# Hybrid decoder layer on one Trainium2 core: the last attention block is normalised ahead of a scan and two gelus, and the output projection starts three chunks at once

## The chip, the cores and the metric

The kernel runs on one core of one Trainium2 chip. That core has five engines with a queue each: TensorE (PE, with its weight loads shown as PEld), VectorE (DVE), ScalarE (ACT), GpSimd (POOL) and SyncE (SP), which here only issues transfers. [...] The metric is the time of one execution in microseconds of the device.

## The reference

One layer: a half-step SwiGLU FFN, a token mixer made of two channel groups that run side by side, and a second half-step FFN, each between two RMS norms. The change lies in the mixer, at the place where its two groups come together:

```python
def rg_lru(x_in, ...):
    xc = causal_depthwise_conv(x_in, conv_w, conv_b)
    r = sigmoid(block_diag(xc, w_rg, b_rg)); i = sigmoid(block_diag(xc, w_ig, b_ig))
    log_a = LRU_C * r * log_sigmoid(lam)
    a = exp(log_a);  u = sqrt(-expm1(2.0 * log_a)) * (i * xc)
    h = associative_scan(h_t = a_t * h_{t-1} + u_t)          # along the sequence

y_lru  = rg_lru(x_lru, ...) * gelu(gate_lru)                  # 512 channels
y_attn = sliding_window_sink_attention(q, k, v, sinks)        # 512 channels, 8 heads of 64, blocks of 128
y = concatenate([rms_norm(y_lru, g_lru_out), rms_norm(y_attn, g_attn_out)])
return y @ w_o                                                # 1024 -> 1024
```

Sizes: 512 tokens, 1024 channels, FFN width 2816, one layer, float32.

## The kernel before

Activations lie transposed, 128 channels on the partitions by 512 tokens, one tile per chunk of channels. A float32 product is made of three passes of TensorE: weight and activation are each split into a high part (rounded by a ScalarE copy or activation) and a low part (the difference, made by VectorE or GpSimd), and high by high, high by low and low by high are summed in a bank of PSUM. `x_high` (line 431) and `x_low` (line 434) do this for an activation, and the planner `Weights` does it for weights: `W.take()` hands out a split weight, `W.fill(n)` splits ahead, and the next raw weight is fetched when the last user of a raw buffer has been issued. One low part of the output weight, `Deferred` (line 157), is written down at once but issued later by hand, with `deferred.run()`. The order on all five engines is the order of the program's calls.

The mixer's middle runs in ten steps, `now` from 0 to 9. There are eight units (block `b` of 128 queries, `n` one of two groups of four heads); in step `now` unit `now` gets its scores and exponentials, unit `now - 1` its transposed probabilities (`turn_p`), and unit `now - 2` its product with the values (`values`). With `n == 1` `values` ends a block: the reciprocal of the softmax sums (line 1268), the scaled output `yn` of the block (line 1271, from PSUM), and, deferred by `later` to a `run_due`, the sum of its squares on ScalarE (line 1273). Between these steps `pump(n)` puts pieces of the gate's projection `gt0` to `gt3` on TensorE, and the recurrent group's elementwise work goes on: `root`, `root_u`, the four `scan(ci)` (line 1172, VectorE), and the gelu of gate chunk `ci` in four parts: `gelu_a` scales it by the RMS factor (line 1012) and squares it (line 392), `gelu_b` makes the inner polynomial (lines 1120 and 1121), `gelu_c` the tanh (line 1124), `gelu_d` the product (line 1128, tile `G`). `G` exists for chunks 0 and 1; for 2 and 3 the product with the gate and that with 1 + tanh (`gated`, line 1354) stand apart.

Behind the loop, in the kernel before: `invert_rms` turns the sums of squares into 1/rms, by a root on ScalarE (line 1278, which needs another table of functions than tanh and exp), a reciprocal (line 1279) and one VectorE multiplication per block (line 1281); `turn_y` puts 16 TensorE transposes of the four normalised blocks into four banks `atp` (line 1331) and splits each bank into `yah` and `yal`; GpSimd multiplies the scans by the gates (line 1357); `gated` and `add_square` (lines 1342 and 1344) make the sum of squares `acc_lru`, which `lrms.stats()` takes to TensorE (line 406). `wo_attn(c)` (lines 1374 to 1377) starts output chunk `c` of `w_o` with the attention half alone: per chunk eight passes with `yah` and four with `yal`. Three chunks come ahead of `lrms.stats()`, two behind it; the recurrent half follows when its norm is known (line 1392 and line 361 on).

`preload(f)` is an activation on one dummy column that makes ScalarE load a table early (line 337).

Of the kernel before, what the change touches and what calls it, by code (L numbers as in the profile page):

```python
# [9 lines left out]
F32R = mybir.dt.float32r  # L10
U8 = mybir.dt.uint8
AF = mybir.ActivationFunctionType
# [3 lines left out]
P = 128  # L16
T = 512
NB = T // P
D = 1024
KD = D // P  # L20
F = 2816
FC = F // P
C = 512
KC = C // P
# [9 lines left out]
PUMPS = [(2, 1)] * 8 + [(1, 1), (1, 0), (4, 0)]  # L34
# [77 lines left out]
def tile_layer(ctx: ExitStack, tc: tile.TileContext, out: bass.AP, **ins: bass.AP):  # L112
    nc = tc.nc
    pe, dve, act, pool, sync = nc.tensor, nc.vector, nc.scalar, nc.gpsimd, nc.sync
# [10 lines left out]
    ALL = slice(0, T)  # L125
    HALF = [slice(0, T // 2), slice(T // 2, T)]

    def bank(name):
        return psum.tile([P, T], F32, tag="bank", name=name)

    def t2k(name, dt=F32):
        return big.tile([P, T], dt, tag="t2k", name=name, bufs=NT2K)

    def wt(name, w=T, dt=F32):
        return tmp.tile([P, w], dt, tag="w", name=name, bufs=NW)
# [184 lines left out]
    ident = const.tile([P, P], F32, name="ident")  # L320
# [11 lines left out]
    eps = filled("eps", 1, EPS)  # L332
# [3 lines left out]
    def preload(func):  # L336
        act.activation(dummy, eps, func)
# [9 lines left out]
    def col(name, i):  # L347
        return colrange(name)[:, i:i + 1]
# [41 lines left out]
    def square(src, sl, name):  # L390
        sq = wt(f"sq_{name}")[:, sl]
        act.activation(sq, src, AF.Square)  # L392
        return sq
# [36 lines left out]
    def x_high(x, src, gain, sl):  # L430
        act.activation(x[0][:, sl], src, AF.Copy, scale=gain)

    def x_low(x, src, gain, sl):
        dve.scalar_tensor_tensor(x[1][:, sl], src, gain, x[0].bitcast(F32)[:, sl], op0=ALU.mult, op1=ALU.subtract)
# [359 lines left out]
    ws = [w_tiles(KD, P, f"first{i}") for i in range(2)]  # L794
# [37 lines left out]
    tps = turn_early()  # L832
# [3 lines left out]
    banks = [bank(f"a_first{i}") for i in range(4)]  # L836
# [44 lines left out]
    tps = {c: turn(1, c) for c in range(0, KD, 2)}  # L881
# [87 lines left out]
    for g, (f0, f1) in enumerate(GROUPS1):  # L969
# [3 lines left out]
        for c in range(KD):  # L973
# [19 lines left out]
            b = pair_banks[c] if c < 2 else product(W.take(), xs, name=f"ya{g}{c}")  # L993
# [17 lines left out]
    def scaled(t, b):  # L1011
        dve.tensor_mul(t, b, R)
        return t
# [68 lines left out]
    for j in range(4):  # L1082
        b = in_product(f"pq{j}")
# [14 lines left out]
    Gs = {}  # L1098
# [3 lines left out]
    def later(i, fn, *args):  # L1102
        todo.append((i, fn, args))

    def run_due(i):
        nonlocal todo
        due, todo = [t for t in todo if t[0] <= i], [t for t in todo if t[0] > i]
        for _, fn, args in due:
            fn(*args)


    gts, gqs = {}, {}
# [5 lines left out]
    def gelu_b(ci):  # L1118
        sq = gqs[ci]
        dve.tensor_scalar(sq, sq, GC * GA, GC, op0=ALU.mult, op1=ALU.add)  # L1120
        (dve if ci else pool).tensor_mul(sq, sq, gts[ci])

    def gelu_c(ci):
        act.activation(gqs[ci], gqs[ci], AF.Tanh)
# [21 lines left out]
    now = 0  # L1146
    steps = fill_steps()

    def pump(n):
        for _ in range(n):  # L1150
            next(steps, None)
# [11 lines left out]
    def root(ci):  # L1163
        act.activation(th[ci], th[ci], AF.Sqrt)
# [4 lines left out]
    hl = us_  # L1169

    def scan(ci):
        dve.tensor_tensor_scan(hl[ci], rs_[ci], us_[ci], initial=0.0, op0=ALU.mult, op1=ALU.add)


    scale = HD ** -0.5
    yns = []
    ssq = const.tile([P, NB], F32, name="ssq")
# [76 lines left out]
    def values(b, n):  # L1254
        pc, pp = unit[b, n]
        if n == 0:
            unit[b, "o"] = bank(f"po{b}")
        po = unit[b, "o"]
        for j in range(4):
            hs = slice(j * P, (j + 1) * P)  # L1260
            o = po[:, (4 * n + j) * HD:(4 * n + j + 1) * HD]
            if b > 0:
                pe.matmul(o, pp[:, hs], v[:, (b - 1) * P + n * HD:(b - 1) * P + (n + 1) * HD], start=True, stop=False)
            pe.matmul(o, pc[:, hs], v[:, b * P + n * HD:b * P + (n + 1) * HD], start=b == 0, stop=True)
        if n == 0:
            return
        rden = small.tile([P, 8], F32, tag="rden", name=f"rden{b}")
        dve.reciprocal(rden, unit[b])
        yn = t2k(f"yn{b}")
        h8 = lambda t: t.rearrange("p (h d) -> p h d", h=8)  # L1270
        dve.tensor_mul(h8(yn), h8(po), rden.unsqueeze(2).to_broadcast([P, 8, HD]))
        yns.append(yn)
        later(now, lambda: act.activation(wt(f"junk{b}"), yn, AF.Square, accum_out=ssq[:, b:b + 1]))

    rat = const.tile([P, NB], F32, name="rat")

    def invert_rms(bs):
        act.activation(rat[:, bs], ssq[:, bs], AF.Sqrt, bias=eps, scale=1.0 / C)
        dve.reciprocal(rat[:, bs], rat[:, bs])
        for b in range(NB)[bs]:  # L1280
            dve.tensor_scalar(yns[b], yns[b], rat[:, b:b + 1], None, op0=ALU.mult)
# [6 lines left out]
    for now in range(n_units + 2):  # L1288
        if now < n_units:
            scores(*units[now])  # L1290
            if now in FILLS:
                W.fill(FILLS[now])
        pump(PUMPS[now][0])
        if 0 <= now - 1 < n_units:
            turn_p(*units[now - 1])
        if now < n_units:
            exps(*units[now])
        if now == 0:
            deferred.run()
        run_due(now - 1)  # L1300
        pump(PUMPS[now][1])
        if 0 <= now - 2:
            values(*units[now - 2])
        if now == 5:
            for ci in range(KC):
                root(ci)
            preload(AF.Exp)
        if now == 6:
            for ci in range(KC):
                root_u(ci)  # L1310
            for ci in (2, 3):
                scan(ci)
        if now == n_units:
            scan(0)
            deferred.run()
            scan(1)
            gelu_b(2)
            gelu_c(2)


    pump(PUMPS[-1][0])
    invert_rms(slice(0, NB - 1))
    run_due(n_units + 1)
    invert_rms(slice(NB - 1, NB))
    ysp = [None] * KD

    def turn_y():
        tps = [bank(f"atp{ci}") for ci in range(KC)]
        for b in range(NB):
            for ci in range(KC):  # L1330
                pe.transpose(tps[ci][:, b * P:(b + 1) * P], yns[b][:, ci * P:(ci + 1) * P], ident)
        for ci, tp in enumerate(tps):
            ysp[ci + KC] = t2k(f"yah{ci}", F32R), t2k(f"yal{ci}", F32R)
            x_high(ysp[ci + KC], tp, col("g_attn_out", ci), ALL)
            x_low(ysp[ci + KC], tp, col("g_attn_out", ci), ALL)


    accl = tmp.tile([P, T], F32, tag="acc", name="acc_lru", bufs=3)
# [1 line left out]
    def add_square(ci):  # L1340
        if ci == 0:
            act.activation(accl, hl[0], AF.Square)
        else:
            dve.tensor_add(accl, accl, square(hl[ci], ALL, f"l{ci}"))

    pump(100)
    gts[KC - 1] = scaled(wt(f"gt{KC - 1}"), gts[KC - 1])
    turn_y()
    gqs[KC - 1] = square(gts[KC - 1], ALL, f"g{KC - 1}")
    preload(AF.Exp)  # L1350
    gelu_b(KC - 1)

    def gated(ci):
        dve.scalar_tensor_tensor(hl[ci], gqs[ci], 1.0, hl[ci], op0=ALU.add, op1=ALU.mult)

    for ci in range(KC):
        pool.tensor_mul(hl[ci], hl[ci], Gs[ci] if ci in Gs else gts[ci])
    gated(2)
    for ci in (0, 1):
        add_square(ci)  # L1360
    gelu_c(3)
    gated(3)
    for ci in (2, 3):
        add_square(ci)
    preload(AF.Sqrt)
    lrms = [InvRms([accl], mean_c, h, f"lru{h}", eps4) for h in range(2)]
# [1 line left out]
    res = Residual("r2", lambda c: col("mix_post_g", c))  # L1368
    EARLY = KD - LATE

    def wo_attn(c):
        (hi, lo), ks = ws[c], range(KC, KD)
        for k in ks:
            pe.matmul(banks[c], hi[:, k, :], ysp[k][0], start=k == KC, stop=False)
            pe.matmul(banks[c], lo[:, k, :], ysp[k][0], start=False, stop=False)
        for k in ks:
            pe.matmul(banks[c], hi[:, k, :], ysp[k][1], start=False, stop=False)

    ws, banks = [], []
    for c in range(EARLY):  # L1380
        ws.append(W.take(0))
        banks.append(bank(f"wo{c}"))
        wo_attn(c)
        if c == EARLY - 3:
            for l in lrms:
                l.stats()
            W.fill(3)
        if c == EARLY - 2:
            bcs = [l.spread() for l in lrms]
            for ci in range(KC):  # L1390
                for h in range(2):
                    dve.tensor_mul(hl[ci][:, HALF[h]], hl[ci][:, HALF[h]], bcs[h])
                y = t2k(f"ylh{ci}", F32R), t2k(f"yll{ci}", F32R)
                x_high(y, hl[ci], col("g_lru_out", ci), ALL)
                x_low(y, hl[ci], col("g_lru_out", ci), ALL)
                ysp[ci] = y
# [12 lines left out]
    banks = boundary(res, late, ysp, None, n2, "m")  # L1409
# [46 lines left out]
    for tb in range(NB):  # L1456
        end = tb == NB - 1
        pieces = [(0, 0, T)] + ([(1, 0, T // 2), (1, T // 2, T)] if end else [(1, 0, T)])
        banks = [bank(f"ybl{tb}{i}") for i in range(len(pieces))]
# [5 lines left out]
        for i, f in steps:  # L1465
            dh, c0, c1 = pieces[i]
            if (i, f) == (1, f0):

                tp = []
# [63 lines left out]
```

## Time and profile before

| | |
|---|---|
| median of three runs | 889.82 us (888.49 to 889.88) |
| the profiled execution | 888.32 us, of which its span is 886.6 us |
| mean granted TensorE clock over the span | 0.996 |
| VectorE, ScalarE and GpSimd busy in 450 to 460 us | 9.27, 9.79 and 4.54 of 10.00 us |
| the same in 460 to 470 us | 9.78, 4.06 and 6.75 of 10.00 us |
| the same in 470 to 480 us | 7.27, 6.22 and 3.76 of 10.00 us, TensorE 6.49 at a clock of 0.83 |
| HBM over the span | 83.67 MB read, 97 GB/s |

Times within the execution are microseconds from the start of the span. The chain of waits follows the work that ended last back from the last instruction; the timeline lists an engine's instructions with their durations, merging neighbours of one line ("x2"). Two neighbours on one engine may overlap by some 0.08 us in it.

### The profile page before, as it was taken

What the parts mean: (1) busy time and instruction counts of PE and PEld (TensorE: products, weight loads), DVE (VectorE), ACT (ScalarE), POOL (GpSimd) and SP (SyncE); (2) the same over time, 40 slices, a digit from 0 to 9 for tenths busy, and PEclk for the clock granted to TensorE, in tenths of its full rate; (3) what the DMA queues carried; (4) which work ended last, traced back from release to release, by engine and by line L of the source; (5) the groups of instructions that cost most, each with busy time, mean ns of one, the idle gap of its engine ahead of it and who ended that gap; (6) DMA issues with size and microseconds to landing.
All of it is one profiled execution on the core that took longest, in us unless ns stands there. A gap on an engine that the chain in (4) does not pass through costs nothing.

```text
span 886.6 us, 14242 instructions
## 1 busy us (share of the span) xinstructions
PE 874.6 (99%) x5768; PEld 801.9 (90%) x5768; DVE 668.3 (75%) x993; ACT 459.0 (52%) x790; POOL 127.7 (14%) x117
## 2 busy tenths in 40 slices
PE   9999999999999999999998999999999999999997
PEld 8989989989989998988886899888998998998996
DVE  5979768678678855989897679588677677777754
ACT  6656534545535544547785356535463462552542
POOL 2010000000000015426462054210000000000013
PEclk9999999999999999999999999999999999999999
DMA  7243152242242253232201140224232241261212
GB/s 239 91 148 107 61 167 72 72 143 72 78 138 96 84 175 109 74 96 96 95 1 48 50 141 2 96 95 143 95 121 71 96 143 48 96 190 37 90 42 95
DMA packets 83553, 86.68 MB, mean 98 GB/s; under 512 B 3664, under 2 KB 75680, under 8 KB 83488
## 3 DMA queue, kind: packets, MB, share of 16 engines
q1 hardware_dynamic: 83312, 85.64, 29.7%
q8 instruction: 45, 0.74, 0.3%
q14 instruction: 20, 0.16, 0.1%
q10 hardware_dynamic: 144, 0.13, 0.0%
q0 software_dynamic: 32, 0.00, 0.0%
HBM read 83.67 MB, written 2.10 MB: 97 GB/s over the span
## 4 chain that ended last, share of the span: by engine, by line
PE 93%; DVE 4%; ACT 1%; issue 1%; POOL 0%; POOLq 0%; DVEq 0%; ACTq 0%
PE aa L676 12%; PE ab L676 10%; PE da L676 6%; PE db L676 5%; PE ya L361 4%; PE ya L363 4%; PE ya L362 4%; PE yb L1417 4%; PE yb L1418 4%; PE yb L1419 4%; PE ba L676 3%; PE bb L676 3%; PE a_first L841 1%; PE an L380 1%; PE mn L380 1%; PE mn L387 1%
## 5 line engine op out<-in xcount | busy, mean ns | idle before, releaser
L361 PE MATMUL ya<-hha,whi_ad 128*128 128x512 f32 x158 | 61.5, 389 | 0.0
L362 PE MATMUL ya<-hla,whi_ad 128*128 128x512 f32 x158 | 61.5, 389 | 0.0
L363 PE MATMUL ya<-hha,wlo_ad 128*128 128x512 f32 x158 | 61.5, 389 | 0.0
L1417 PE MATMUL yb<-whi_bd,hhb 128*128 128x512 f32 x144 | 56.1, 389 | 0.0
L1418 PE MATMUL yb<-wlo_bd,hhb 128*128 128x512 f32 x144 | 56.1, 389 | 0.0
L1419 PE MATMUL yb<-whi_bd,hlb 128*128 128x512 f32 x144 | 56.0, 389 | 0.0
L1487 POOL TENSOR_TENSOR yp_b<-yp_b,grow 128x512 f32<-128x512 f32 (+1 forms) x8 | 9.7, 1221 | 282.0 <-ACT ysq L1481 282.0
L942 POOL MEMSET bd_w_rg<- 128x512 f32 x1 | 0.5, 527 | 265.5 <-PE aa L676 265.5
L363 PEld LDWEIGHTS ya<-hha,wlo_ad 128*128 128x128 f32 x158 | 29.7, 188 | 6.2
L362 PEld LDWEIGHTS ya<-hla,whi_ad 128*128 128x128 f32 x158 | 29.7, 188 | 6.0
L361 PEld LDWEIGHTS ya<-hha,whi_ad 128*128 128x128 f32 x158 | 29.7, 188 | 6.0
L1419 PEld LDWEIGHTS yb<-whi_bd,hlb 128*128 128x128 f32 x144 | 27.0, 188 | 5.7
L1417 PEld LDWEIGHTS yb<-whi_bd,hhb 128*128 128x128 f32 x144 | 27.0, 188 | 5.5
L1418 PEld LDWEIGHTS yb<-wlo_bd,hhb 128*128 128x128 f32 x144 | 27.0, 188 | 5.5
L176 DVE TENSOR_TENSOR wlo_bd<-raw_bd,whi_bd 128x1024 fp32r<-128x1024 f32 x22 | 26.4, 1219 | 3.6 <-ACT whi_bd L171 3.6
L171 ACT CAST whi_bd<-raw_bd 128x1024 fp32r<-128x1024 f32 x22 | 22.9, 1049 | 5.1 <-PE bb L676 2.5
L1438 DVE TENSOR_TENSOR yp_b<-yb,yp_b 128x512 f32<-128x512 f32 x24 | 16.4, 692 | 11.6 <-PE yb L1419 11.6
L1000 DVE TENSOR_TENSOR yp_a<-ya,yp_a 128x512 f32<-128x512 f32 x24 | 16.4, 687 | 8.8 <-PE ya L363 8.8
L697 DVE TENSOR_TENSOR p1a<-p1a,ba 128x512 f32<-128x512 f32 x9 | 6.2, 688 | 21.7 <-PE ba L676 21.7
L697 DVE TENSOR_TENSOR p1b<-p1b,bb 128x512 f32<-128x512 f32 x8 | 5.5, 688 | 18.2 <-PE bb L676 18.2
L380 PE MATMUL an<-xh_mx,whi_xl 128*128 128x256 f32 x64 | 15.9, 289 | 0.0
L527 POOL TENSOR_TENSOR acca_r<-acca_r,sq_r 128x512 f32<-128x512 f32 x6 | 8.4, 1404 | 50.4 <-ACT sq_r L392 50.4
(1524 smaller groups left out, 3424.7 us busy)
## 6 DMA issues: line engine op xcount, KB each, us to landing
raw_bd<-in_ffn_w_down SPq DMA_DIRECT2D x10, 1024.0 KB, 6.7
xn<-in_x SPq DMA_DIRECT2D x8, 256.0 KB, 4.2
raw_q<-in_w_in SPq DMA_DIRECT2D x4, 512.0 KB, 3.7
out_dram<-yp_b SPq DMA_DIRECT2D x7, 256.0 KB, 2.0
first<-in_ffn_w_gu SPq DMA_DIRECT2D x4, 256.0 KB, 4.7
raw_second<-in_ffn_w_gu SPq DMA_DIRECT2D x2, 512.0 KB
raw_ag__104<-in_ffn_w_gu SPq DMA_DIRECT2D x1, 1024.0 KB
raw_au__286<-in_ffn_w_gu SPq DMA_DIRECT2D x1, 1024.0 KB, 5.7
```

What stands on the lines that cost most here:

```text
L171: act.copy(two(hi, x), x)
L176: low.tensor_sub(two(lo, x), x, two(hi.bitcast(F32), x))
L361: pe.matmul(ps, hi[:, k, :], xh, start=start, stop=False)
L362: pe.matmul(ps, hi[:, k, :], xl, start=False, stop=False)
L363: pe.matmul(ps, lo[:, k, :], xh, start=False, stop=stop)
L380: pe.matmul(ps[:, sl], hi[:, k, :], xh, start=k == 0, stop=False)
L676: pe.matmul(o, w[:, k, js], x, start=first and i + j + k == 0, stop=k == 3 and i == 2, skip_group_check=True)
L1000: dve.tensor_add(parts[c], b, parts[c])
L1417: pe.matmul(ps, hh[:, blk], hi[:, k, cs], start=start, stop=False)
L1418: pe.matmul(ps, hh[:, blk], lo[:, k, cs], start=False, stop=False)
L1419: pe.matmul(ps, hl_[:, blk], hi[:, k, cs], start=False, stop=stop)
L1438: dve.tensor_add(parts[tb, dh], ybanks[tb], parts[tb, dh])
```

## The change

The arithmetic of every tile stays as it is; what moves is the order, and with it what each engine does in the last two steps and behind the loop.

- In step 8, `scan(1)`, `gelu_b(2)` and `gelu_c(2)` go; a preload of the root's table and the root over the first three blocks' sums of squares come in their place.
- The last block's sum of squares is issued at once in `values`, and its root right behind the loop; then a preload of the table of exp and tanh.
- `invert_rms` (now the reciprocal and the multiplications alone) runs for all four blocks at once, and only then `scan(1)`, the rest of the gate's projection and the scaling of gate chunk 3.
- The transposes go bank by bank and no longer block by block. ScalarE splits each bank's high part as it comes (with the square of gate chunk 3 behind the second); VectorE makes the low parts of banks 0 and 1, then `gelu_b` of chunks 2 and 3, then the low parts of banks 2 and 3; the two tanh follow on ScalarE.
- GpSimd's products go in the order 0, 2, 1, 3; both `gated` come ahead of all four `add_square`.
- `wo_attn` takes a list of chunks: the first three are done together, bank `yah` by bank, and their twelve passes with `yal` come last.

```diff
-        later(now, lambda: act.activation(wt(f"junk{b}"), yn, AF.Square, accum_out=ssq[:, b:b + 1]))
+        sum_of = lambda: act.activation(wt(f"junk{b}"), yn, AF.Square, accum_out=ssq[:, b:b + 1])
+        if b < NB - 1:
+            later(now, sum_of)
+        else:
+            sum_of()
...
+    def root_rms(bs):
+        act.activation(rat[:, bs], ssq[:, bs], AF.Sqrt, bias=eps, scale=1.0 / C)
+
     def invert_rms(bs):
-        act.activation(rat[:, bs], ssq[:, bs], AF.Sqrt, bias=eps, scale=1.0 / C)
         dve.reciprocal(rat[:, bs], rat[:, bs])
...
         if now == n_units:
             scan(0)
             deferred.run()
-            scan(1)
-            gelu_b(2)
-            gelu_c(2)
-
-
-    pump(PUMPS[-1][0])
+            preload(AF.Sqrt)
+            root_rms(slice(0, NB - 1))
+
+
+    root_rms(slice(NB - 1, NB))
+    preload(AF.Exp)
     invert_rms(slice(0, NB - 1))
+    invert_rms(slice(NB - 1, NB))
+    scan(1)
     run_due(n_units + 1)
-    invert_rms(slice(NB - 1, NB))
+    pump(100)
     ysp = [None] * KD
...
+    gts[KC - 1] = scaled(wt(f"gt{KC - 1}"), gts[KC - 1])
+    tps = [bank(f"atp{ci}") for ci in range(KC)]
+    for ci, tp in enumerate(tps):
         for b in range(NB):
...
+            pe.transpose(tp[:, b * P:(b + 1) * P], yns[b][:, ci * P:(ci + 1) * P], ident)
+        ysp[ci + KC] = t2k(f"yah{ci}", F32R), t2k(f"yal{ci}", F32R)
+        x_high(ysp[ci + KC], tp, col("g_attn_out", ci), ALL)
+        if ci == 1:
+            gqs[KC - 1] = square(gts[KC - 1], ALL, f"g{KC - 1}")
+    for ci in (0, 1):
+        x_low(ysp[ci + KC], tps[ci], col("g_attn_out", ci), ALL)
+    for ci in (2, 3):
+        gelu_b(ci)
+        gelu_c(ci)
+    for ci in (2, 3):
+        x_low(ysp[ci + KC], tps[ci], col("g_attn_out", ci), ALL)
...
+    for ci in (0, 2, 1, 3):
+        pool.tensor_mul(hl[ci], hl[ci], Gs[ci] if ci in Gs else gts[ci])
+    for ci in (2, 3):
+        gated(ci)
     for ci in range(KC):
...
         add_square(ci)
...
+    def wo_attn(cs):
+        ks = range(KC, KD)
         for k in ks:
...
+            for c in cs:
+                for part in ws[c]:
+                    pe.matmul(banks[c], part[:, k, :], ysp[k][0], start=k == KC and part is ws[c][0], stop=False)
+        for c in cs:
+            for k in ks:
+                pe.matmul(banks[c], ws[c][0][:, k, :], ysp[k][1], start=False, stop=False)
...
     for c in range(EARLY):
         ws.append(W.take(0))
         banks.append(bank(f"wo{c}"))
-        wo_attn(c)
+        if c < EARLY - 3:
+            continue
+        wo_attn(range(c + 1) if c == EARLY - 3 else [c])
         if c == EARLY - 3:
             for l in lrms:
                 l.stats()
```

More of the change, by code (lines that the diff above doesn't have):

```diff
@@ L1315, in tile_layer @@
             deferred.run()
-            scan(1)
-            gelu_b(2)
-            gelu_c(2)
-    pump(PUMPS[-1][0])
+            preload(AF.Sqrt)
+            root_rms(slice(0, NB - 1))
+    root_rms(slice(NB - 1, NB))
+    preload(AF.Exp)
     invert_rms(slice(0, NB - 1))
+    invert_rms(slice(NB - 1, NB))
+    scan(1)
     run_due(n_units + 1)
-    invert_rms(slice(NB - 1, NB))
+    pump(100)
     ysp = [None] * KD
-    def turn_y():
-        tps = [bank(f"atp{ci}") for ci in range(KC)]
+    gts[KC - 1] = scaled(wt(f"gt{KC - 1}"), gts[KC - 1])
+    tps = [bank(f"atp{ci}") for ci in range(KC)]
+    for ci, tp in enumerate(tps):
         for b in range(NB):
[L1330 to L1335, printed above, removed]
+            pe.transpose(tp[:, b * P:(b + 1) * P], yns[b][:, ci * P:(ci + 1) * P], ident)
[10 more added lines that the diff above has]
+        x_low(ysp[ci + KC], tps[ci], col("g_attn_out", ci), ALL)
     accl = tmp.tile([P, T], F32, tag="acc", name="acc_lru", bufs=3)
@@ L1344, in add_square @@
             dve.tensor_add(accl, accl, square(hl[ci], ALL, f"l{ci}"))
[L1346 to L1351, printed above, removed]
     def gated(ci):
         dve.scalar_tensor_tensor(hl[ci], gqs[ci], 1.0, hl[ci], op0=ALU.add, op1=ALU.mult)
+    for ci in (0, 2, 1, 3):
+        pool.tensor_mul(hl[ci], hl[ci], Gs[ci] if ci in Gs else gts[ci])
+    for ci in (2, 3):
+        gated(ci)
     for ci in range(KC):
[L1357 to L1363, printed above, removed]
         add_square(ci)
@@ L1369, in tile_layer @@
     EARLY = KD - LATE
-    def wo_attn(c):
-        (hi, lo), ks = ws[c], range(KC, KD)
+    def wo_attn(cs):
+        ks = range(KC, KD)
         for k in ks:
[L1374 to L1377, printed above, removed]
+            for c in cs:
[4 more added lines that the diff above has]
+                pe.matmul(banks[c], ws[c][0][:, k, :], ysp[k][1], start=False, stop=False)
     ws, banks = [], []
```

## The prediction

> **What bounds the kernel now.** First the page: TensorE is busy for nearly the whole span, so time can only come out of its few gaps or its clock.
>
> ```profile
> span 886.6 us, 14242 instructions
> ...
> PE 874.6 (99%) x5768; PEld 801.9 (90%) x5768; DVE 668.3 (75%) x993; ACT 459.0 (52%) x790; POOL 127.7 (14%) x117
> ```
>
> Then the busy time per stretch around the change's place (columns: stretch, its length, then busy us of each engine, the granted TensorE clock, DMA share, GB/s).
>
> ```profile
> 466.00:470.60 4.60, 4.60 (x26) 3.67 (x25) 4.57 (x6) 0.38 (x3) 2.18 (x1) 1.00 0.52 164
> 470.60:474.00 3.40, 0.03 (x2) 0.04 (x1) 2.47 (x6) 2.94 (x6) 2.48 (x2) 1.00 0.26 91
> 474.00:477.60 3.60, 3.47 (x16) 3.07 (x16) 1.80 (x6) 0.73 (x2) 1.27 (x1) 0.53 0.00 0
> 477.60:480.10 2.50, 2.49 (x9) 1.56 (x10) 2.50 (x4) 2.48 (x5) 0.00 (x0) 1.00 0.00 0
> ```
>
> TensorE stands still for 3.4 us between the last pass of `gt3` and the first transpose, and then runs 16 transposes at a clock of 0.53. Four transposes of this size (line 1244) take 0.44 us at full clock, so 16 need 1.76; the eight `yah` passes of the first chunk need 8 x 0.228 = 1.82 (a later chunk's, 481.00 to 482.84, is 1.84). From 470.62 to 480.08 pass 9.46 us for 3.58 us of work: the bubble is worth 5.9 us at most.
>
> Third, the chain of waits through that place (start, length, what):
>
> ```profile
> 467.12 2.23 DVE xc L1172
> 469.35 0.33 DVE sq_g L1120
> ...
> 469.70 0.70 DVE sq_g L1121
> ...
> 470.43 0.63 ACT sq_g L1124
> ...
> 471.08 0.88 ACT L1278
> ...
> 472.37 0.30 ACT rat L1278
> ...
> 472.91 0.94 DVE yn L1281
> ...
> 473.99 2.86 PE atp L1331 x13
> ...
> 476.87 0.70 ACT yah L431
> ```
>
> The attention's norm waits behind `scan(1)`, the gelu of chunk 2 and a table load, none of which it needs. Last the timelines of VectorE and of GpSimd:
>
> ```profile
> 465.92 1.20 DVE L157 TENSOR_TENSOR wlo_wo<-raw_wo__4578,whi_wo 128x1024 fp32r<-128x1024 f32 x1
> 467.04 2.31 DVE L1172 TENSOR_TENSOR_SCAN xc<-r,xc 128x512 f32<-128x512 f32 x1
> ...
> 471.21 0.69 DVE L1271 TENSOR_TENSOR yn<-po,rden 128x512 f32<-128x512 f32 x1
> ...
> 472.91 1.73 DVE L1281 TENSOR_SCALAR yn<-yn,rat 128x512 f32<-128x512 f32 x3
> ```
>
> ```profile
> 466.09 2.18 POOL L1357 TENSOR_TENSOR xc<-xc,G 128x512 f32<-128x512 f32 x1 [1.38 <-DVE xc L1172]
> ...
> 471.08 1.26 POOL L1357 TENSOR_TENSOR xc<-xc,G 128x512 f32<-128x512 f32 x1 [2.81 <-DVE G L1128]
> 472.30 1.26 POOL L1357 TENSOR_TENSOR xc<-xc,gt 128x512 f32<-128x512 f32 x1
> ```
>
> The two engines take turns where both read SBUF: GpSimd's first product (2.18 for 1.26) runs only when the weight's low part ends at 467.1, and the scan behind it (2.31; the other undisturbed one, at 464.79, 1.22) only when the product ends at 468.27. `yn`, which reads PSUM, takes its usual 0.69 wholly inside a product.
>
> **The change part by part.** Up to 467.12 nothing moves. From there, in times of this execution:
>
> *VectorE to the last `yn`.* `scan(1)` and `gelu_b(2)` (2.23 + 0.33 + 0.70) leave this path; `G1` (0.61 a step) takes the scan's slot and, I take it, its wait for the product: 468.27 + 0.6 = 468.9. Reciprocal and `yn` of block 3: 0.99 as at 470.92 to 471.91, so 469.9. If VectorE won the turn instead, all this is 1.15 earlier; the row in the same slot says it loses.
>
> *ScalarE.* It idles from 466.2 to 470.43. The root's table (1.28), dummy (0.2) and root over three blocks (0.30) fit in there, by 468.0; the load of 471.08 thus leaves the path. Behind `yn` come the last sum (0.61 + 0.19, less overlap, as 472.57 to 473.28) and root: 470.9. The other table load, at 479.83 before, now stands ahead of the first `yah`: 470.9 + 1.28 + 0.2 = 472.3.
>
> *Norm and transposes.* Reciprocal 0.2, then four multiplications of 0.4 with one reciprocal between: 1.95, plus 0.15 of waiting for the product of chunk 2 (now 468.9 to 470.1): last `yn` at 472.0. The first bank's transposes follow each multiplication (470.6, 471.0, 471.4, 472.1); the other 12 take 1.3, to 473.4. Bank 0 is complete at 472.3, just as ScalarE is free; `yah0` takes 0.70, to 473.0, the others 0.61 each with a square of 0.52 between, so every 1.37 us that six passes need one is there. First output pass: 473.4, against 477.61.
>
> TensorE's gap is then three pieces of 0.3 to 0.7 us. The 3.38 us gap cost a clock of 0.53 behind it; 0.49 us of idling in 510 to 520 us cost nothing (clock 1.00). I take nothing, by the nearer row; the other end is 1.7 us (3.4 us at half speed). [...]
>
> *Output passes.* The 36 of three chunks, 8.2 us, are the same in number; done bank by bank they lose the 0.65 us that the first eight lost to `yah`. They end at 481.6; before, the sum of squares went to TensorE at 486.46 right behind them.
>
> *The recurrent tail, hidden under these passes.* VectorE from 472.0: `scan(1)` 1.13, `gt3` 0.65, two `yal` 1.36 (PSUM, so beside GpSimd's products of 1 and 3, 473.1 to 475.6): 475.1. Then `gelu_b` of 2 waits for the product's end: 475.6, and both take 2 x 1.08: 477.8. Two `yal`: 479.1, in time for the low passes at 478.9 + 0.5. The tanh (0.63 each) lie under these. Two `gated`: 480.4; three additions of 0.6, the squares of 0.62 just ahead: 482.2. This cover is short: the sum is 0.6 late, and TensorE waits. Sum of squares at 482.2 instead of 486.46: **4.3 us earlier.** ScalarE's last table load, from 480.9, is through at 482.4, and TensorE's first sums need 0.38 (486.46 to 486.84): no further wait.
>
> *Behind that* all offsets stay: the weights' casts, low parts and `spread` are issued from the same point. No transfer's trigger moves against its user: the load at 467.15 hangs on the low part that ends at 467.12, as before; the next wait for buffers freed behind the sums, their weights are used some 17 us later (490.8 to 513.2), so they have cover. In 520 to 840 us TensorE has no gap, so the gain lasts to the end.
>
> Sum: the profiled execution's 888.32 (span 886.6 plus 1.7 around it) less 4.3 is 884.0. It lies 1.5 below the median, and the four executions shown average 889.13; from there 884.8. I say **885.0**.
>
> Ends: port won, gain 5.4; everything hidden, 5.9: 883.2 from the average. Half clock after the short gaps, or low parts that wait for GpSimd after all (1.26 each at most), gain 2.6 to 3: about 886.5. Both, or three more turns lost of about 1 us, gain 1.5: 887.6.
>
> **Rivals.**
>
> *A, VectorE becomes the bound* (gain 1.8 to 3.7; 885.4 to 887.3, say 886.5). For it: it is filled from 467 to 482 without a gap, and the sum is late already. Against: its reads of PSUM are shown not to wait.
>
> *B, given back, or no effect* (889.1, within 1.8 us): the stretch ends as early as I say, but something behind it has its own time, a load above all; or the norm waits for what I did not see. For: DMA engines are 0.64 busy in 520 to 530. Against: the 17 us of cover, and clean removal of 3.3 us of VectorE work from the chain.
>
> *C, slower: the clock drops in the new order of passes.* The 24 `yah` passes change bank every second pass, with small gaps ahead. At half clock each pass costs 0.23 more: 24 cost 5.5, all 36 cost 8.2. From (4.3 + 1.8) / 0.228 = 27 passes on it is slower by over 0.2%; all 36 give 889.1 - 4.3 + 8.2 = 893.0. Against it stands the same order over four banks (line 380) in a stretch at full clock:
>
> ```profile
> 528.00:557.00 29.00, 29.00 (x219) 27.87 (x218) 25.90 (x53) 15.49 (x35) 12.40 (x13) 1.00 0.11 35
> ```
>
> [...]
>
> **How the numbers follow.** Forecast 0.72, A 0.18, B 0.06, C 0.04. 0.2%, 1.8 us, is about what a measurement of this kernel can tell from no change. Forecast and A together are faster: 0.90; B the same: 0.06; C slower: 0.04. The range 883.0 to 887.6 holds the forecast's ends and nearly all of A; the forecast's own is 883.0 to 886.0.
>
> **What would show it.** Right: idle time before the first transpose under 1.6 us instead of 3.4; clock 1.00 in the transposes; first output pass near 473.4; `G1` taking about 1.8 us from 467.04; `yal` at 0.74 beside GpSimd's products; `scan(1)` behind `yn`; the sum of squares on TensorE near 482.2, with up to 0.6 us of waiting for `acc_lru`; later stages shifted by the same amount. Wrong: a clock under 1 behind the short gaps, `yal` of 1.3 or more, output passes that wait for a high part, or a shift that shrinks behind 490 us.

## The result, and the profile after

The changed kernel takes 884.86 us (median of six runs, 884.58 to 886.51) against 889.34 us for the kernel before on the same chip (six runs, 888.49 to 890.05): a ratio over all runs of 0.9957 with a 95% interval of 0.9947 to 0.9966. The two medians differ by 4.5 us; the ratio stands for 3.8 us, and its interval for 3.0 to 4.7. The prediction said 885.0. The profiled execution of the changed kernel is one of its two slower runs, 886.26 us with a span of 884.6, for a reason at its start that is shown below.

The head of its page:

```profile
span 884.6 us, 14243 instructions
...
PE 873.8 (99%) x5768; PEld 801.5 (91%) x5768; DVE 668.5 (76%) x993; ACT 459.5 (52%) x791; POOL 129.0 (15%) x117
```

The engines' busy time is what it was (TensorE 0.8 us less, ScalarE 0.5 and GpSimd 1.3 us more). The stretches around the change, with the same columns as before:

```profile
466.00:470.60 4.60, 4.60 (x32) 4.17 (x32) 4.60 (x5) 2.92 (x6) 3.23 (x3) 1.00 0.10 22
470.60:474.00 3.40, 3.06 (x15) 1.99 (x14) 3.23 (x10) 2.25 (x4) 1.26 (x1) 1.00 0.82 283
474.00:477.60 3.60, 3.60 (x23) 3.20 (x22) 3.60 (x5) 3.19 (x7) 2.54 (x2) 1.00 0.00 0
477.60:480.10 2.50, 2.50 (x12) 2.07 (x12) 2.43 (x6) 1.27 (x3) 0.00 (x0) 1.00 0.00 0
480.10:486.50 6.40, 5.67 (x29) 4.53 (x28) 5.04 (x12) 5.23 (x10) 0.00 (x0) 1.00 0.01 1
```

The stretch in which TensorE did 0.03 us of work is gone, and the clock is 1.00 in every row, the last included, where TensorE misses 0.73 us. VectorE is now nearly full too: up to 480.1 us it misses 0.24 us of 14.1, TensorE 0.34.

All of this lies 1.88 us later than in the profile of before, because this execution started slowly:

```profile
4.00:8.00 4.00, 2.82 (x17) 2.19 (x16) 0.94 (x3) 1.47 (x4) 0.00 (x0) 1.00 0.88 267
8.00:12.00 4.00, 4.00 (x18) 3.72 (x19) 3.18 (x8) 3.00 (x7) 0.22 (x1) 0.57 1.12 339
```

TensorE waits for the first loads between 4 and 8 us and then runs at a clock of 0.57. So two profiles are compared here by a part of the span, called the *stretch* from now on: from the end of VectorE's low part of the output weight (`wlo_wo`, line 157; 467.12 before, 469.00 after) to the start of the first sum of squares on TensorE (`rms_lru`, line 406). It is 19.18 us before and 15.20 after: 3.98 us. From that sum to the last pass of the kernel it is 394.05 us before and 394.11 after, so nothing is given back.

The chain of waits through the stretch (start, length, what):

```profile
469.00 1.71 DVE G L1128
...
470.92 0.69 DVE yn L1271
...
471.73 1.28 DVE yn L1287 x3
...
473.60 1.13 DVE xc L1172
...
475.31 1.31 DVE yal L434 x2
476.63 1.01 DVE sq_g L1120
...
479.46 0.63 ACT sq_g L1124
480.09 0.53 ACT acc_lru L1356
...
481.38 1.24 ACT sq_l L392 x2
...
484.20 1.05 PE rms_lru L406 x8
```

Before, this chain ran through the scan, a gelu, a table load, the transposes and `yah`; now it is VectorE's own queue up to 479.4 us. Behind that the view passes twice through ScalarE, through the second tanh and through the squares, but VectorE's timeline has no idle time over 0.15 us there either: the two engines end within 0.15 us of each other in both places. Two of VectorE's pieces in it are longer than their work: `G` and the polynomial of line 1120. Their timelines, VectorE's and then GpSimd's:

```profile
468.91 1.79 DVE L1128 SCALAR_TENSOR_TENSOR G<-sq_g,gt 128x512 f32<-128x512 f32 x1
...
475.23 1.40 DVE L434 SCALAR_TENSOR_TENSOR yal<-atp,cols,yah 128x512 fp32r<-128x512 f32 x2
476.55 1.09 DVE L1120 TENSOR_SCALAR sq_g<-sq_g 128x512 f32<-128x512 f32 x1
...
478.27 0.42 DVE L1120 TENSOR_SCALAR sq_g<-sq_g 128x512 f32<-128x512 f32 x1
```

```profile
467.96 2.19 POOL L1364 TENSOR_TENSOR xc<-xc,G 128x512 f32<-128x512 f32 x1 [1.38 <-DVE xc L1172]
470.12 1.75 POOL L1364 TENSOR_TENSOR xc<-xc,gt 128x512 f32<-128x512 f32 x1
474.81 1.29 POOL L1364 TENSOR_TENSOR xc<-xc,G 128x512 f32<-128x512 f32 x1 [2.95 <-DVE xc L1172]
476.06 1.29 POOL L1364 TENSOR_TENSOR xc<-xc,gt 128x512 f32<-128x512 f32 x1
```

`G` waits for the first product, and the polynomial (0.42 alone, 1.09 here) ends 0.3 us behind the end of the last one, while the two `yal` beside the products take 1.40, as the later two with no product beside them do. What TensorE waits for, in its timeline:

```profile
473.65 1.64 PE L1338 MATMUL atp<-ident,yn 128*128 128x128 f32 x13 [0.27 <-DVE yn L1287]
...
484.20 1.05 PE L406 MATMUL rms_lru<-mean_c,acc_lru 128*128 128x1 f32 x8 [0.73 <-DVE acc_lru L1358]
```

One gap of 3.38 us has become 0.27 and 0.73.

### The profile page after: what moved, and what is told of

It is laid out like the page before. It is cut to its first block, busy times and chain, and to the rows that moved or that the text cites. A ratio compares the mean times of both kernels' runs of the same rounds, so it can differ in the third digit from the quotient of the medians.

```text
span 884.6 us, 14243 instructions
## 1 busy us (share of the span) xinstructions
PE 873.8 (99%) x5768; PEld 801.5 (91%) x5768; DVE 668.5 (76%) x993; ACT 459.5 (52%) x791; POOL 129.0 (15%) x117
## 4 chain that ended last, share of the span: by engine, by line
PE 91%; DVE 5%; ACT 2%; issue 1%; DMA 1%; POOL 0%; SPq 0%; POOLq 0%; DVEq 0%; ACTq 0%
PE aa L676 12%; PE ab L676 10%; PE da L676 6%; PE db L676 5%; PE ya L361 4%; PE ya L362 4%; PE ya L363 4%; PE yb L1426 4%; PE yb L1427 4%; PE yb L1425 4%; PE ba L676 3%; PE bb L676 3%; PE a_first L841 1%; PE an L380 1%; PE mn L380 1%; PE mn L387 1%
## 5 line engine op out<-in xcount | busy, mean ns | idle before, releaser
L381 PE MATMUL an<-xh_mx,wlo_xl 128*128 128x256 f32 x64 | 15.5, 283 | 0.0
```

## The experiments

Twelve runs were made; e10_after_again repeats the changed kernel and e12_square_again repeats e9_square_early. Ratios are to the kernel before on the same chip, and the small times given for an event in the stretch count from the end of `wlo_wo`. "Wait" is TensorE's largest in the stretch.

| run | time, us (median, range) | ratio, 95% | stretch | wait |
|---|---|---|---|---|
| before | 889.34 (888.49 to 890.05) | | 19.18 | 3.38 |
| after | 884.86 (884.58 to 886.51) | 0.9957 (0.9947 to 0.9966) | 15.20 | 0.73 |
| e1_spin | 890.39 | 1.0022 (1.0011 to 1.0033) | 20.83 | 0.45 (the gap is overfilled) |
| e8_spin13 | 887.48 (887.01 to 889.22) | 0.9991 (0.998 to 1.0002) | 17.94 | 0.45 |
| e2_wo_by_chunk | 887.74 (886.62 to 888.88) | 0.9995 (0.9985 to 1.0005) | 17.60 | 1.69 |
| e3_scan_back | 887.44 (885.9 to 887.8) | 0.998 (0.997 to 0.999) | 18.22 | 1.49 |
| e6_g1_behind | 885.46 (884.28 to 887.53) | 0.9967 (0.9955 to 0.9979) | 15.27 | 1.06 |
| e4_pool_order | 886.66 (885.67 to 887.84) | 0.9976 (0.9966 to 0.9986) | 16.18 | 1.08 |
| e5_lows_first | 885.0 (884.67 to 886.65) | 0.9963 (0.9952 to 0.9974) | 15.26 | 0.79 |
| e7_best | 884.73 (884.29 to 885.6) | 0.9961 (0.9948 to 0.9975) | 14.28 | 0.47 |
| e9_square_early | 884.46 (884.13 to 885.11) | 0.9955 (0.9943 to 0.9967) | 13.87 | 0.16 |
| e10_after_again | 884.85 (884.6 to 885.33) | 0.996 (0.9947 to 0.9973) | 15.22 | 0.69 |
| e11_poly_back | 884.4 (884.02 to 886.12) | 0.9948 (0.9935 to 0.9961) | 14.92 | 0.78 |
| e12_square_again | 884.65 (884.13 to 884.98) | 0.9948 (0.9935 to 0.9962) | 13.98 | under 0.1 |

### How much of the gain is the clock behind the gap

In the kernel before, passes on the identity fill the gap, and nothing else is changed:

```diff
         tps = [bank(f"atp{ci}") for ci in range(KC)]
+        for _ in range(26):
+            pe.matmul(tps[KC - 1][:, :P], ident, ident, start=True, stop=True)
         for b in range(NB):
```

> The kernel before, with 26 idle 128x128 matmuls on TensorE (into a bank that the transposes overwrite) between the last pass of gt3 and the first transpose; nothing else is changed, and the output is the same. The stretch from the end of the weight's low part (line 157) to the first sum of squares on TensorE was 19.34 us before and is 15.20 with the whole change. My theory: 1.4 us of the gain is the clock that fell behind the 3.38 us gap. Then the clock reads 1.00 in the transposes, the 13 of the chain take 1.4 to 1.5 us instead of 2.86, the stretch is 17.9 to 18.1 us, and the time 1.2 to 1.5 us under the kernel before. Rival: the transposes are slow because of what they wait for or write, not because of the gap; then they keep 2.8 us, and the stretch stays at 19.3.

The clock stayed at 1.00, but each of these float32 products is two passes of 0.11 us, where a transpose of the same size is one: the 26 overfilled the gap and pushed the transposes back. Inconclusive, so it was repeated with 13:

> The run with 26 idle matmuls again, with 13: each turned out to be two passes of 0.11 us, so 26 of them overfilled the gap of 3.38 us, and 13 fill 2.9 of it. From here on the stretch is counted from the end of the weight's low part to the start of the first sum's instruction: 19.18 us before, 15.20 with the whole change, 20.83 with 26 idle matmuls. Theory: with the clock kept at 1.00 the transposes behind the multiplications take 1.4 to 1.6 us instead of 3.1, the stretch is 17.6 to 18.0 us and the time 1.2 to 1.5 us under the kernel before; the rest of the change's gain (2.4 us or more) is the idle gap itself and the first output passes. Rival: the transposes stay slow, stretch 19.2.

The stretches of e8_spin13 that hold the filled gap, and then the transposes:

```profile
471.00:474.40 3.40, 3.40 (x30) 3.28 (x29) 2.46 (x6) 3.00 (x6) 2.51 (x2) 1.00 0.31 109
474.40:476.60 2.20, 2.01 (x19) 1.73 (x17) 1.86 (x5) 0.48 (x1) 0.22 (x1) 1.00 0.00 0
```

VectorE and ScalarE have the queues of the kernel before, yet the transposes run at 1.00 instead of 0.53, and the stretch is 17.94 instead of 19.18. So in the profiled execution 1.24 us of the change's 3.98 are the clock that the gap cost; the other 2.7 are waiting that went. The theory's 17.6 to 18.0 held. The time alone does not show it, since the interval of the ratio reaches to no change (1.0002): the kernel before does not run at the same mean clock in every execution. In the 73 executions of it beside these experiments, the 16 with a mean granted clock of 0.998 or 0.999 took 886.9 to 887.6 us, and the 26 with 0.994 or 0.995 took 889.1 to 890.6. Seven of the ten executions of e8_spin13 show 0.998 or 0.999 and took 887.0 to 887.6, as the former do. The changed kernel at this clock took 884.6 to 885.3 (ten executions of after and e10_after_again), about 2.5 us less, near the 2.7 of waiting. The mean clock does not say at which place it fell, so this supports the split and does not prove it.

### What the order of the output passes is worth

```diff
-        if c < EARLY - 3:
-            continue
-        wo_attn(range(c + 1) if c == EARLY - 3 else [c])
+        wo_attn([c])
```

> The changed kernel with the output passes chunk by chunk again (eight passes with the high parts and four with the low parts per chunk). My theory: the order of passes is what hides VectorE's work between the low parts of banks 1 and 3; without it the first chunk's low passes wait for the last low part (end 480.74 in the changed kernel's profile, where these passes would be due near 478.3), and 24 passes of 0.228 us still follow it. TensorE then waits 2 to 2.6 us there, the stretch grows from 15.20 to 17.2 to 17.8 us, and the time by 2.0 to 2.6 us. Rival: the passes' order matters little, because TensorE waits for the sum of squares anyway; then the stretch grows by under 0.8 us.

One line of TensorE's timeline tells it:

```profile
478.38 0.50 PE L1383 MATMUL wo<-yal,whi_wo 128*128 128x512 f32 x1 [1.69 <-DVE yal L434]
```

Chunk by chunk, the third and fourth `yal` are wanted at 9.43, and VectorE has them at 11.1 and later, behind two polynomials. The stretch is 17.60 and the ratio to before 0.9995: without the passes that come bank by bank, most of what the early norm wins is lost again. The theory's 17.2 to 17.8 held for the stretch. Its executions fall in two groups: five at 886.6 to 887.3 us with a mean clock of 0.999, and five at 888.2 to 888.9 with 0.996 or 0.997.

### Where the second scan stands

```diff
             scan(0)
             deferred.run()
+            scan(1)
             preload(AF.Sqrt)
...
-    scan(1)
     run_due(n_units + 1)
```

> The changed kernel with scan(1) back in step 8, ahead of the last block's softmax division and norm. VectorE's whole work in the stretch is the same. My theory: since TensorE waits 0.73 us for the sum of squares behind the passes, VectorE's total sets the end, and a norm 1.1 us later is mostly swallowed: the gap before the last transposes grows from 0.27 to 1.3 to 1.5 us, the clock stays at 1.00, the wait for the sum shrinks to nothing, and the stretch grows by 0.3 to 0.6 us. Rival: the norm's time is the bound, and its whole delay of 1.1 to 1.2 us is paid: the stretch is 16.3 us or more.

The theory fell: the stretch is 18.22, and the delay of 3.0 us is more than the 1.1 to 1.2 that its rival named. VectorE's timeline in e3_scan_back, and then GpSimd's:

```profile
467.44 2.30 DVE L1172 TENSOR_TENSOR_SCAN xc<-r,xc 128x512 f32<-128x512 f32 x1
469.67 1.72 DVE L1128 SCALAR_TENSOR_TENSOR G<-sq_g,gt 128x512 f32<-128x512 f32 x1
```

```profile
466.49 2.17 POOL L1364 TENSOR_TENSOR xc<-xc,G 128x512 f32<-128x512 f32 x1 [1.16 <-DVE xc L1172]
468.62 2.21 POOL L1364 TENSOR_TENSOR xc<-xc,gt 128x512 f32<-128x512 f32 x1
```

The scan waits for the first product, the second product waits for the scan, and `G` then waits for the second product: each engine gets the next turn of the other, and VectorE pays twice. The four multiplications end at 6.87 instead of 4.61. TensorE, which in after had work up to the first transposes, now waits 1.49 us for them (the 0.27 before the last ones stays, at 0.26), and the clock behind it drops again:

```profile
471.50:473.30 1.80, 0.31 (x2) 0.14 (x1) 1.67 (x4) 0.88 (x3) 1.23 (x1) 1.00 0.21 70
...
475.30:478.80 3.50, 3.50 (x14) 3.01 (x12) 3.17 (x6) 3.11 (x6) 1.05 (x1) 0.51 0.00 0
```

So moving one scan of 1.13 us is worth 3.0 us of the stretch: its own slot, a lost turn, and the clock.

### Taking the other waiter out of the path

`G1` is issued behind `scan(1)` and no longer ahead of the norm:

```diff
-        run_due(now - 1)
+        if now <= n_units:
+            run_due(now - 1)
```

> The changed kernel with the gelu product G1 behind scan(1), no longer ahead of the last block's yn. G1 loses 1.1 us there because GpSimd's first product has the turn; yn reads PSUM and does not need the turn, so yn comes 1.6 to 1.7 us earlier. My theory of turns: the wait only moves on. The first multiplication of the norm waits for the same product, and the second one for GpSimd's next product, which now takes its turn in between; scan(1) and all behind it end within 0.3 us of where they were, and the stretch stays at 15.0 to 15.5 us. Rival: the wait is filled by yn and gone; then VectorE ends about 1 us earlier, TensorE's wait of 0.73 us for the sum of squares vanishes, and the stretch is 14.4 to 14.6 us.

```profile
468.93 1.97 DVE L1287 TENSOR_SCALAR yn<-yn,rat 128x512 f32<-128x512 f32 x3
```

The turn is lost all the same, now by the first multiplication (1.18 us for 0.48, while GpSimd's second product runs from 1.11 to 2.40). `yn` came 1.2 us earlier and not 1.6 to 1.7, because it then waited 0.58 us for TensorE's product. The stretch is 15.27, within what the theory of turns said. The norm is done 0.5 us sooner, but the additions hold the sum where it was, so TensorE waits 1.06 instead of 0.73; and this wait, unlike that of after, is followed by half clock:

```profile
480.00:484.70 4.70, 3.63 (x21) 2.83 (x20) 3.43 (x10) 3.78 (x7) 0.00 (x0) 1.00 0.00 2
484.70:488.10 3.40, 3.40 (x10) 2.63 (x9) 2.57 (x4) 1.23 (x2) 0.00 (x0) 0.50 0.00 0
```

From the sums to the last pass it is 395.69 here instead of 394.01 to 394.16 where the clock stayed: 1.6 us for 0.33 us of more waiting. This execution is not every one: four of the eight show a mean clock of 0.998 or 0.999 and took 884.3 to 884.7 us, and four show 0.996 or 0.997 and took 886.2 to 887.5.

### The order of GpSimd's products

```diff
-    for ci in (0, 2, 1, 3):
+    for ci in range(KC):
```

> The changed kernel with GpSimd's products in the order 0, 1, 2, 3. Theory of turns: the product of chunk 2 no longer uses the time before scan(1) has ended, so GpSimd is busy until about 9.6 us into the stretch instead of 8.35, VectorE's inner polynomials lose a second turn of 1.2 to 1.3 us, and the sum of squares is ready at 16.3 to 16.5: stretch 16.3 to 16.7, with a wait of 1.8 to 2.1 us in front of it. Rival: GpSimd's order is off the path; stretch within 0.3 us of 15.20.

The wait was 1.08, under what was expected, because the passes themselves ended later (0.15 us for a late `yal`); the sum came 0.98 us later, 16.18, a little under the expectation too. In this order GpSimd still works at 9.8 and not only until 8.4, and the second gelu's product on VectorE (line 1121) takes 1.66 us instead of 0.69. Half clock followed here as well, and 395.73 us to the end.

### What holds the sum of squares: VectorE or ScalarE

The four low parts come ahead of the two polynomials:

```diff
-    for ci in (0, 1):
+    for ci in range(KC):
         x_low(ysp[ci + KC], tps[ci], col("g_attn_out", ci), ALL)
...
-    for ci in (2, 3):
-        x_low(ysp[ci + KC], tps[ci], col("g_attn_out", ci), ALL)
```

> The changed kernel with all four attention low parts (they read PSUM) ahead of the two inner polynomials (they do not), so that GpSimd's last product runs beside the low parts. Theory of turns: the polynomial's 0.7 us of waiting is gone, the sum of squares is ready 0.4 to 0.6 us earlier, TensorE's wait of 0.73 shrinks to 0.1 to 0.3, and the stretch is 14.6 to 14.8. Rival: the tanh behind the polynomials, now later, set the end; stretch 15.2 or more.

The theory fell, and its rival came true. The wait of the polynomial for GpSimd's turn is gone (0.42), but the sum does not move (15.26). ScalarE's timeline in e5_lows_first:

```profile
479.08 0.63 ACT L1124 ACTIVATE sq_g<-sq_g 128x512 f32<-128x512 f32 x1 [1.96 <-DVE sq_g L1121]
480.14 0.63 ACT L1124 ACTIVATE sq_g<-sq_g 128x512 f32<-128x512 f32 x1 [0.43 <-DVE sq_g L1121]
480.68 0.62 ACT L1354 ACTIVATE acc_lru<-xc 128x512 f32<-128x512 f32 x1
481.20 1.66 ACT L392 ACTIVATE sq_l<-xc 128x512 f32<-128x512 f32 x3
```

The squares of chunks 0 and 1 need no tanh, yet stand in ScalarE's queue behind both; the first addition waits for them. Two kernels take this up. The first joins the edits of e5_lows_first and e6_g1_behind and moves the polynomials of chunks 2 and 3 to ScalarE, as an activation with a bias tile `gcol`; the second also puts GpSimd's product of chunk 0 and its square ahead of the norm (both shown in part):

```diff
+    gcol = filled("gcol", 1, GC)
...
-        dve.tensor_scalar(sq, sq, GC * GA, GC, op0=ALU.mult, op1=ALU.add)
+        if ci < 2:
+            dve.tensor_scalar(sq, sq, GC * GA, GC, op0=ALU.mult, op1=ALU.add)
...
+    for ci in (2, 3):
+        act.activation(gqs[ci], gqs[ci], AF.Identity, bias=gcol, scale=GC * GA)
```

```diff
     preload(AF.Exp)
+    accl = tmp.tile([P, T], F32, tag="acc", name="acc_lru", bufs=3)
+    pool.tensor_mul(hl[0], hl[0], Gs[0])
+    act.activation(accl, hl[0], AF.Square)
     invert_rms(slice(0, NB - 1))
...
-    for ci in (0, 2, 1, 3):
+    for ci in (2, 1, 3):
```

> The changed kernel with three edits: the low parts first (as in the run beside this one), G1 behind scan(1), and the scaling and shift inside the polynomial (line 1120, chunks 2 and 3) moved from VectorE to ScalarE, behind its four high parts; the arithmetic is the same. Theory: VectorE's tail is then 1.2 us or more shorter than the passes, no wait is left in front of the sum of squares, and the passes alone set the stretch, 14.1 to 14.5 us; the time is 0.7 to 1.1 us under the changed kernel, more if the wait had cost the clock in some executions. Rival: ScalarE becomes the bound with the two added operations, stretch 15 or more.

> The run with three edits, and a fourth: the square of chunk 0 of the recurrent half on ScalarE moves from behind the two tanh to the idle time ahead of the first high part (its input is ready at 1.2 us into the stretch). In the run without it the sum of squares was late by 0.47 us, and its first addition waited for that ScalarE queue (two squares behind two tanh). Theory, ScalarE's queue: the additions start 0.35 us or more earlier, the wait falls from 0.47 to 0.15 us or less, the stretch from 14.28 to 13.8 to 14.0 us, and the time is some 1.2 us under the changed kernel run beside it. Rival, VectorE's chain of additions is what is late: the stretch stays within 0.1 us of 14.28.

> The changed kernel as it is, on the same chip as the run beside it, for a comparison in one place: stretch 15.2 us, time 3.5 to 4.5 us under the kernel before. Its executions should fall in groups some 1.7 us apart, by whether the clock was halved for 3.4 us at the start or behind the wait for the sum of squares.

Both theories held for the length of the stretch: 14.28, though with a wait of 0.47 before the sum where none was expected, then 13.87 with none there; in e9_square_early the sums follow the passes without a releaser in their line:

```profile
482.25 0.94 PE L406 MATMUL rms_lru<-mean_c,acc_lru 128*128 128x1 f32 x7
```

But against after on the same chip (e10_after_again, whose six runs all lay between 884.6 and 885.33, without the second group that was expected) the time is only 0.4 us lower where some 1.2 were expected, and the ranges overlap. In e7_best and e9_square_early TensorE waits 0.72 and 0.69 us from 22.3 and 22.6 us of the span, long before the steps that these edits reorder, and `wlo_wo` ends at 468.15 and 468.39 instead of 467.29.

### What the added constant costs at the start

> e9_square_early without its added constant: the two polynomials of the gelu go back to VectorE. e7_best and e9_square_early, the two kernels with that constant, wait 0.72 and 0.69 us at 22.4 to 22.6 us from the start (TensorE, for the first xh_a behind its late loads), and their low part of wo's weight ends at 468.15 and 468.39 instead of 467.29 in e10_after_again. Theory (the constant does it): here the wait is under 0.1 us and that low part ends at 467.1 to 467.5. Rival (it is scatter of the first loads): the wait may be here or not, and e12_square_again differs from e9_square_early. The stretch from that low part to the sums should be 14.2 to 14.9 by either (e5_lows_first 15.26 less about 0.4 for the early square, less what GpSimd's freed turn gives).

> e9_square_early once more, unchanged. Theory (the constant): the wait of 0.6 to 0.8 us at 22 to 23 us is there again and the low part of wo ends at 468.1 to 468.5. Rival (scatter): the wait is under 0.3 us or gone, and the low part ends near 467.3. The stretch is 13.8 to 13.9 by both, and the time 884.2 to 884.8 by the theory, 883.5 to 884.2 by the rival if its start is undisturbed in most runs.

The repeat shows the wait again (0.70), and the kernel without the constant does not have it. Its profile alone proves little, since that execution was late at the start and reached this place 0.75 us after e9_square_early; but no other kernel here has the wait either, e10_after_again with its quick start among them. `wlo_wo` ends at 468.06 in e12_square_again, just under what was expected; in e11_poly_back it ends at 469.07, which is no measure of this, since that execution had 3.4 us of half clock at 9.36 like the one of after. The stretches are 14.92 and 13.98, both a little above what was expected. The loads tell the cause's place. From 9 to 12 us, in e12_square_again and then in e10_after_again:

```profile
9.00:12.00 3.00, 3.00 (x27) 3.00 (x26) 2.51 (x7) 1.87 (x4) 0.61 (x1) 1.00 1.16 291
```

```profile
9.00:12.00 3.00, 3.00 (x28) 3.00 (x27) 3.00 (x8) 2.42 (x5) 0.81 (x1) 1.00 1.15 351
```

With DMA engines equally full they bring 291 GB/s instead of 351, and the second weight is rounded 0.9 us later (13.92 and 13.01). All profiles divide in this way: 291 to 294 GB/s in these 3 us for the three with the constant, 341 to 352 for the eleven without. Why is open. In the program's allocation `gcol` moves the tiles of the first loads by 32 bytes: the first weight's tile starts at byte 106528 of a partition instead of 106496. No run here shows whether that is the cause, because none shifts the tiles alone. So the constant is shown to cost the start, and the shift as its cause is only the author's guess.

On its chip e11_poly_back took 884.4 and e12_square_again 884.65: the runs cannot tell these two apart. Both beat the kernel before; over after, 0.4 us is all that was measured.

## Why the prediction was right

Times of the profile of after are given less 1.88, so that they stand on the prediction's axis.

- **Bound.** Right: TensorE's gap of 3.38 us and the half clock behind it are what was won. In the profiled executions the gain splits into 1.24 us of clock (e8_spin13) and 2.74 us of waiting. Of the waiting, the order of the passes and the scan's place were put back singly (e2_wo_by_chunk, e3_scan_back); what the gelu of chunk 2 and the table load were worth by themselves was not run.
- **VectorE to the last `yn`.** `G1` loses its turn and ends at 468.82 (said 468.9); block 3's `yn` ends at 469.73 (469.9). What the prediction's ends call a port is this turn: the runs show waits of such a length, not what makes them.
- **ScalarE.** The root's table and root stand in its idle time (468.10 to 469.79 in the profile); the other table load ends at 472.17 and its dummy at 472.38 (472.3).
- **Norm and transposes.** The last multiplication ends at 471.72 (472.0): the 0.15 us of waiting for the product of chunk 2 did not occur; the first multiplication started 0.14 us ahead of that product's recorded end. First output pass 473.17 (473.4).
- **Clock behind the short gaps.** "I take nothing" held: 1.00 throughout. But the margin was thin: 1.06 us at the same place cost 1.6 us in the profile of e6_g1_behind. That no cost came is in part luck, since the prediction had no row between 0.49 and 3.38 us of idling. It took short gaps to be free from the row with 0.49 us alone; e3_scan_back, e4_pool_order and e6_g1_behind show half clock behind 1.06 to 1.49 us of idling.
- **Output passes.** 36 passes end at 481.58 (481.6).
- **The recurrent tail.** The polynomial's wait for GpSimd came as said, and both `gelu_b` end at 477.54 (477.8). `yal` were undisturbed, and the last ends at 478.87 (479.1); both `gated` end at 480.06 (480.4). The three additions, though, took 2.2 us from there and not 1.8: each reads the sum of the one before, and they start at 481.86, 482.65 and 483.45 in the profile, 0.8 us apart and not 0.6. They end at 482.26 (482.2), so that two misses of 0.3 and 0.4 us cancel. TensorE waited 0.73 us for the sum (0.6).
- **The sum.** 482.32 against 482.2 is 0.12 us late, and the sum's start before is 486.30 by its instruction where the chain showed 486.46: 3.98 us instead of 4.3. The direction and the order of the waits held; these 0.3 us and the additions were mis-sized.
- **Behind that.** 394.05 and 394.11 us to the last pass: rival B (given back) did not occur. (The two times that the prediction gives for the cover there, 490.8 and 513.2, are 22.4 us apart and not 17; it says the same with either.) Rival C did not either: the 24 passes over three banks ran at 1.00. Rival A did not occur in its size (a gain of 1.8 to 3.7), but its engine sets the end of the stretch now, by the 0.73 us that TensorE waits: VectorE, and close behind it ScalarE (e5_lows_first).

The medians differ by 4.5 us, the stretch by 4.0, and the interval of the ratio, 3.0 to 4.7 us, holds both. The kernel before scatters from 886.9 to 890.6 over the chips used, at mean granted clocks from 0.999 down to 0.994. The prediction took 4.3 us from a mean of four such executions; that 885.0 came within 0.14 us of the median is therefore luck, and what is confirmed is the 4 us and where they come from.

## What to carry to other kernels

When an engine waits at a join, look at what stands ahead of the needed instruction in the *other* engines' queues: here a scan, a gelu and a table load stood ahead of a norm that needed none of them. Price such an operation by more than its length: putting one scan of 1.13 us back cost 3 us, with a lost turn and a lower clock behind it. After such a change little work is left to cover the next bound, so this has to be measured again: here it was first VectorE's, then ScalarE's order, and a constant of four bytes in each partition took back at the start most of what the last edits won.

## What had not been expected of the hardware

- **The clock dropped behind less idling than the prediction had allowed for.** While the kernel's passes ran, half clock lasted 3.41 us (474.18 to 477.59 in before, 8.27 to 11.68 in after), and its edges lie on a grid of 3.41 us: from its start there to the start of the half clock behind the last pass it is 409.60 us in before, 120 times 3.413, and 873.81 in after, 256 times 3.413. Even in the kernel before, the piece of this grid ahead of the half clock (470.77 to 474.18) held 3.22 us of the gap and so was not wholly idle. Half clock followed waits of 1.49 (e3_scan_back), 1.08 (e4_pool_order) and 1.06 us (e6_g1_behind) and, at the start, of 0.47 and 0.71 together (after), 1.04 (e5_lows_first) and 0.77 (e11_poly_back). It did not follow 0.76 us at the start of e3_scan_back, 0.73 (after) or 0.79 us (e5_lows_first) before the sum, nor the 1.69 us of e2_wo_by_chunk, which an edge of the grid cut into 0.75 and 0.94. With smaller waits beside them those two pieces of the grid had 1.21 and 1.09 us of idling, more than some that were followed by half clock. So the time of idling alone does not tell these cases apart, and what does was not shown.
- **A lost turn moved on where no other work filled it.** Taking one waiter out of VectorE's queue made the next instruction that reads a full tile from SBUF wait (e6_g1_behind, 1.18 us for 0.48), and putting another in made two wait (e3_scan_back, the scan 2.30 us for 1.22 and `G` 1.72 for 0.69). Of VectorE's work on full tiles here, what reads PSUM passed beside GpSimd's products at its usual length (in after two `yal` took 1.40 us with the products and 1.40 without); with such work in that place the polynomial's wait went (e5_lows_first, 0.42 us).
- The two passes of a float32 product with the identity (0.11 us each; 26 passes took 3.06 us in e8_spin13) and the slower first loads behind a constant of four bytes in each partition (291 to 294 GB/s from 9 to 12 us, in three profiles out of three) had not been expected either.
